# A hybrid attention layer on one core: the second and third products of every seven-product group change places, and the heads start with the gates

## The chip, the cores and the metric

The kernel runs on one core of one Trainium2 chip. The metric is the device time of one execution in microseconds (us); the time given for a kernel is the median of its runs. TensorE is written PE (its weight loads PEld), VectorE DVE, ScalarE ACT, GpSimd POOL, SyncE SP.

## The reference, cut to what matters

One layer, 256 tokens of 2048 features. The normalised input is multiplied by one wide matrix `w_in`. Its columns give, for each of four token mixers, queries, keys and values of 4 heads of 128, a path `z` and 2048 gate columns; an indexer gives the sparse mixer its top 64 keys.

```python
branches = (o_dsa, o_fox, o_diff, o_dil)          # four attentions, b = 0, 1, 2, 3
for b in range(N_BRANCHES):
    y = branches[b].reshape(bsz, seq, BRANCH_WIDTH) * jax.nn.silu(z_parts[b])
    term = jax.nn.sigmoid(g_parts[b]) * (y @ w_branch[b])
    merged = term if merged is None else merged + term
return x + merged @ w_out                          # then a last RMS norm
```

Everything is float32 and has to be nearly as exact: a matrix product is made of three products of rounded parts.

## The kernel before, in words

**Units.** All large products are cut into units of one weight tile (512 rows x 512 columns, 1 MB, `Raw`) each. `split_hi` (L195, ACT, the instruction at L207) rounds half a tile into `whi`; `split_lo` (L209, DVE, L220) subtracts that from the tile and gives `wlo`. A unit's matmuls (`three`, L378 to L380) take both. There are 8 buffers of `whi` halves and 6 of `wlo` halves, so splits run some three units ahead of PE. Six slots hold the tiles loaded by SP (L174); a slot is freed, and the next tile's load issued, when a tile's last `wlo` half is made.

**The order** is written out by hand: the list `units` (L1125 to L1162) is processed one by one in the loop at L1257. In unit i, for each half, the program issues a `wlo` half of a later unit, a `whi` half of a later unit, then the matmuls of the half. Then come the unit's `post` functions (they read finished PSUM banks), then, in some units, one round of the attention threads, then the threads that begin with this unit. Each engine executes its own instructions in the order in which the program issued them.

**Seven products.** `seven` (L448) computes two neighbouring blocks of 512 columns from 2048 features. Half of the features are handled as a 2 x 2 block product with seven products P1 to P7 (12 matmuls each), the rest by four plain units c2a, c2b, c1a, c1b (24 matmuls each). Four PSUM banks X, Y, Z, W accumulate. P5 uses the tile B12 to which POOL has added B11 by an accumulating DMA (`plus_dram`, L191; L180 to L193 hold `free`, `plus`, `plus_dram`). When P5's last `wlo` half has been made, DVE adds B22 to B12 (`plus`, L187) for P6, and a unit before P7's first split DVE subtracts B12 from B11 (again L187) for P7. P5 writes bank W, ACT reads it (`p5`, L540), then c2a goes on accumulating in W with its second row block (its first row block goes to Z). P3 writes Z.

**Stages.** For each mixer in the order b = 3, 2, 0, 1: one group of seven for queries and keys (`ps_qk`), one for `z` and values (`ps_zv`), two for the 2048 gate columns (`ps_g`, `gate_units`, 22 units), then 16 units that multiply the heads' output by `w_branch` (`ps_b`). At the end comes `w_out` (`ps_o`).

**Threads.** The attention is written as generators. A counter adds a unit's cost (12 in the groups of seven, 24 elsewhere) and a round is run when it has reached the `pace` in force (20; in the gate units 18, for b = 2 15). In a round every active thread goes on to its next `yield`, in the order in which the threads began. `qk_thread` turns queries and keys; `z_thread` makes SiLU(z): a sigmoid on ACT (L625), a product on DVE (L626), then transposes (L609) and copies (L611). `head_thread` and `diff_thread` (b = 2) make one head each: logits (L786), softmax on DVE (L798, L800, L803) with exponentials on ACT (L805), scaling (L821), transposes (L812 to L814), the copy `pt` on ACT (L816), the product with the values (L876 or L908), output `y` and its two parts `yT` (L828, L832, L833). Before, the heads begin right after the queries' group; `ready` (L835) holds them until `qk`, `index`, `fox` and `const` threads have ended, lets the first two heads (for b = 2 the first) go on and the others wait for `z_thread`; `values` (L849) holds a head until `z_thread` has ended. The tag `lg` of the softmax tile has 3 buffers. A unit with `need` first runs the named threads to their end: the first `w_branch` unit needs all heads of its mixer.

Of the kernel before, what the change touches and what calls it, by code (L numbers as in the profile page):

```python
# [112 lines left out]
def body(ctx: ExitStack, tc, x, norm_w, w_in, fox_b_f, lq1, lk1, lq2, lk2, subln_w,  # L113
# [8 lines left out]
    const = ctx.enter_context(tc.tile_pool(name="const", bufs=1))  # L122
# [192 lines left out]
    V = {}  # L315
    FIRST, LAST = 3, 1
# [129 lines left out]
                                    V["sf"][:, t, :, 0].bitcast(F32), op=ALU.subtract)  # L446

    def seven(src, c1, c2, base, ev, name, need={}, start=(),  # L448
              order="P1 P3 P5 c2a P6 c2b P7 P2 c1a P4 c1b", s0=0):

        st = {}
        p0 = 8 - s0
        order = order.split()
        apart = order.index("c2a") < order.index("P5")
        B11 = Raw(src, s0, 4, c1, 512)
        B12 = Raw(src, s0, 4, c2, 512, lead=4)
        B21, B22 = Raw(src, s0 + 4, 4, c1, 512), Raw(src, s0 + 4, 4, c2, 512)
        B12.then = lambda: plus_dram(B12, B11)  # L460

        def whole(half, k0):
            t = slice(half * P, (half + 1) * P)
            return lambda k: (base()[:, k0 + k, 0, t], base()[:, k0 + k, 1, t])

        def product_ps(bank):
            return att_ps(name) if bank == "V" else main_ps(name)

        def form(half, k0):
            return lambda k: (V["sf"][:, half, k0 + k, 0], V["sf"][:, half, k0 + k, 1])  # L470

        def product(bank, act, first=False):
            def mm(u, h):
                if first and h == 0:
                    st[bank] = product_ps(bank)
                for k in (2 * h, 2 * h + 1):
                    three(st[bank], act(k), u, k, first and k == 0, k == 3, on=True)
            return mm

        def plain(k0, two):  # L480
            def mm(u, h):
                for t, bank in enumerate(two):
                    new = bank not in st
                    if new:
                        st[bank] = main_ps(name)
                    act = whole(t, k0)
                    for k in (2 * h, 2 * h + 1):
                        three(st[bank], act(k), u, k, new and k == 2 * h, k == 3, on=True)
            return mm

        def c(k0, c0, two):
            return Unit(Raw(src, k0, 4, c0, 512), plain(k0, two))

        def read(f, bank, last=False):
            def g():
                f(st[bank])
                if last:
                    done(st[bank])
            return g

        def last_of(*names):
            return U[max(names, key=order.index)]

        Q = "V" if apart else "W"
        U = {
            "P1": Unit(B11, product("Y", whole(0, s0), True), [read(ev.p1, "Y")], frees=()),
            "P2": Unit(B21, product("X", whole(0, s0 + 4), True), frees=()),
            "P3": Unit(B22, product("Z", form(0, 4), not apart), frees=()),
            "P4": Unit(B21, product("Y", whole(1, s0 + 4)), frees=[B21], loads=()),
            "P5": Unit(B12, product(Q, form(1, 4), True), [read(ev.p5, Q)], frees=()),  # L510
            "P6": Unit(B12, product("Y", form(0, 0)), [read(ev.u2, "Y")], frees=(), loads=()),
            "P7": Unit(B11, product("Y", form(1, 0)), [read(ev.u3, "Y")], frees=[B11], loads=(),
                       pre=[lambda: plus(B11, B12, ALU.subtract)]),
            "c2a": c(p0, c2, "ZW"), "c2b": c(p0 + 4, c2, "ZW"),
            "c1a": c(p0, c1, "XY"), "c1b": c(p0 + 4, c1, "XY"),
        }
        U["P5"].after.append(lambda: plus(B12, B22))
        last_of("P3", "P5").after.append(lambda: free([B22]))
        last_of("P2", "P6").after += [lambda: plus(B21, B12), lambda: free([B12])]
        last_of("P3", "P6", "c2b").post.append(read(ev.c12, "Z", True))  # L520
        last_of("P7", "c2b", "P2").post.append(read(ev.c22, "W", True))
        U["c1b"].post += [read(ev.c11, "X", True), read(ev.c21, "Y", True)]
        U["c1b"].start += start
        for what, u in U.items():
            u.need += need.get(what, ())
            u.cost = 24 if s0 else 12
        return [U[what] for what in order]
# [57 lines left out]
    def qkvz_units(b, off, scale, start):  # L585


        def tok():
            return big.tile([P, 2, 512], F32, name="tok", tag="g", bufs=4)

        def dst_qk():
            if b == FIRST:
                both = big.tile([P, 2, 2, 512], F32, name="tok2", tag="y")
                V["q_"], V["k_"] = both[:, 0], both[:, 1]
            else:
                V["q_"], V["k_"] = tok(), tok()
            return V["q_"], V["k_"]

        def dst_zv():
            V["z_"] = tok()  # L600
            V["v"] = at.tile([P, 2, 512], F32, name="v", tag="v")
            return V["z_"], V["v"]

        def turn(src, dst, j0):
            for j in range(0, 4, 2):
                tp = att_ps("turn")
                for i in range(2):
                    for t in range(2):
                        nc.tensor.transpose(tp[:, i * S + t * P:i * S + (t + 1) * P],  # L609
                                            src[:, t, (j + i) * P:(j + i + 1) * P], ident)  # L610
                nc.scalar.activation(dst[:, j0 + j:j0 + j + 2],  # L611
                                     tp.rearrange("p (i s) -> p i s", i=2), AF.Copy)
                yield

        def qk_thread():
            V["qk"] = at.tile([P, 8, S], F32, name="qk", tag="qk")
            q_, k_ = V["q_"], V["k_"]
            yield
            yield from turn(q_, V["qk"], 0)
            yield from turn(k_, V["qk"], 4)  # L620

        def z_thread():
            z_ = V["z_"]
            sg = big.tile([P, 2, 512], F32, name="sg", tag="g", bufs=4)
            nc.scalar.activation(sg, z_, AF.Sigmoid)  # L625
            nc.vector.tensor_tensor(z_, z_, sg, op=ALU.mult)  # L626
            yield
            yield
            V["sz"] = at.tile([P, 4, S], F32, name="sz", tag="sz")
            V["v of"] = b  # L630
            yield from turn(z_, V["sz"], 0)

        sc = rsth if scale == HSCALE else rst8
        return (seven(w_in, off, off + 512, lambda: hT, Tok(dst_qk, sc, rst), "ps_qk",
                      start=[("qk", qk_thread)] + start, **(dict(
                          need={"P1": ["stack"], "P3": ["forms"]},
                          order="P1 P2 P3 P5 c2a P6 c2b P7 c1a P4 c1b") if b == FIRST else {}))
                + seven(w_in, O_Z + b * 512, off + 1024, lambda: hT, Tok(dst_zv, rst, rst),
                        "ps_zv", need={"c1b": ["qk"]}, start=[("z", z_thread)]))


    ki_hi = at.tile([P, S], F32R, name="ki_hi")
# [189 lines left out]
        nc.scalar.activation(yT[:, h, 0], y, AF.Copy)  # L832
        nc.vector.tensor_tensor(yT[:, h, 1], y, yT[:, h, 0].bitcast(F32), op=ALU.subtract)  # L833

    def ready(b, h, early):  # L835

        while any(a[0] in ("qk", "index", "fox", "const") for a in active):
            yield
        if h < early:
            for _ in range(2 * h):  # L840
                yield
        else:
            while V.get("v of") != b:
                yield
            for _ in range(h - early):
                yield
                yield

    def values(b):  # L849
        while V.get("v of") != b or any(a[0] == "z" for a in active):  # L850
            yield

    def head_thread(b, h):
        if h == 0:
            V["yT"] = big.tile([P, 4, 2, S], F32R, name="yT", tag="y")
        yield from ready(b, h, 2)
        ps = att_ps("lps")
        logits(ps, h, 0, P)
        if b == 0:
# [6 lines left out]
        nc.vector.reciprocal(r, r)  # L866
        yield
        scaled(e, r)
        yield from values(b)
        yield  # L870
        pt = transposed(e)
        yield
        o = att_ps("o")
        vs = slice(h * P, (h + 1) * P)
        v = V["v"]
# [4 lines left out]
    def diff_thread(b, h):  # L880
        if h == 0:
            V["yT"] = big.tile([P, 4, 2, S], F32R, name="yT", tag="y")
        yield from ready(b, h, 1)
        er = []
        for c in range(2):
            ps = att_ps("lps")
# [10 lines left out]
            nc.vector.scalar_tensor_tensor(e0[:, SL[t]], e1[:, SL[t]], r1[:, t:t + 1],  # L897
                                           e0[:, SL[t]], op0=ALU.mult, op1=ALU.add)
        yield
        yield from values(b)  # L900
        yield
        pt = transposed(e0)
        yield
# [3 lines left out]
        v = V["v"]  # L907
# [11 lines left out]
        for t in range(2):  # L919
            nc.vector.tensor_scalar(on[:, t * P:(t + 1) * P], o[:, t * P:(t + 1) * P],  # L920
                                    ms[:, t:t + 1], 1.0 - LAMBDA_INIT,
                                    op0=ALU.mult, op1=ALU.mult)
        yield
        yield
        yield
        ot = att_ps("otd")
# [211 lines left out]
    for b, off, scale, fn in ((3, O_DIL, HSCALE, head_thread), (2, O_DIFF, 0.125, diff_thread),  # L1138
# [3 lines left out]
        for i in range(2):  # L1142
            units += gate_units(b, i)
        for u in units[-22:]:
            u.pace = 15 if b == 2 else 18
        for n in range(4):
            units += branch_units(b, n)
        if b == 0:
# [7 lines left out]
    for n in range(4):  # L1156
        two[n].need.append(f"merge{n}")
    group = seven(w_out, 0, 512, lambda: V["mT"], Out(), "ps_o", s0=8, need={"P5": ["merge3"]},
                  order="c2a P1 P5 c2b P6 P2 P7 P3 c1a P4 c1b")
# [144 lines left out]
```

## Time and profile before

| | |
|---|---|
| median of 3 runs | 1042.16 us (1042.02 to 1044.82) |
| profiled execution | 1044.16 us, of which the span of the instructions is 1042.4 us |
| mean granted PE clock | 0.966 of full speed |
| busy: PE, DVE, ACT, POOL | 93%, 79%, 61%, 7% of the span |
| HBM | 204 GB/s over the span |

"Busy" of an engine counts its instructions' time; a wait line says which engine and source line waited, for which one, how long in all, how often, and the longest wait. The clock is the share of full speed that the throttle granted to PE.

### The profile page before, as it was taken

Reading aid. Unit: us, or ns where it says so; the run is one execution under the profiler, and the core shown is the slowest. Engines: PE = TensorE matmul, PEld = TensorE weight load, DVE = VectorE, ACT = ScalarE, POOL = GpSimd, SP = SyncE. Lnnn points to the kernel's source line nnn. Section 1 sums busy time; section 2 is a strip of 40 time slices with the busy share of each in tenths; the row PEclk is TensorE's granted clock in tenths of the full one; section 3 lists DMA queues with packets and bytes.
Section 4 is the critical chain, followed back from the end, with each engine's and each line's share of the span. In section 5 each row is a group of like instructions: output and inputs, shape, how many; then the busy total and the mean of one; then the engine's idle time right before and its main releaser. Section 6 shows DMA issues by size and latency. Waiting matters only on the chain. (4 is left out here: it accounts for less than half of the span.)

```text
span 1042.4 us, 12131 instructions
## 1 busy us (share of the span) xinstructions
PE 973.3 (93%) x4443; PEld 799.7 (77%) x4443; DVE 822.7 (79%) x967; ACT 634.7 (61%) x834; POOL 73.0 (7%) x84
## 2 busy tenths in 40 slices
PE   9988998999999989989999979799999797999897
PEld 8866886878878867778788858688788686887776
DVE  5888899978697877597888775887987767869992
ACT  5756676686456667676555665863666567544641
POOL 2011010000010000021100000001000000010220
PEclk9998999999999999989999989899999898999998
DMA  9949484747876938159895574388958562788132
GB/s 321 293 112 286 155 252 136 221 143 243 261 228 228 290 102 242 41 197 280 209 303 161 203 201 162 122 256 222 302 176 275 162 202 81 259 271 317 58 144 81
DMA packets 109019, 213.64 MB, mean 205 GB/s; under 512 B 8083, under 2 KB 10293, under 8 KB 108576
## 3 DMA queue, kind: packets, MB, share of 16 engines
q1 hardware_dynamic: 96240, 181.06, 50.1%
q0 software_dynamic: 12688, 31.80, 14.9%
q8 instruction: 35, 0.57, 0.2%
q14 instruction: 24, 0.20, 0.1%
q10 hardware_dynamic: 32, 0.01, 0.0%
HBM read 204.44 MB, written 8.41 MB: 204 GB/s over the span
## 5 line engine op out<-in xcount | busy, mean ns | idle before, releaser
L207 ACT ACTIVATE whi<-raw 128x1024 fp32r<-128x1024 f32 (+1 forms) x439 | 448.9, 1051 | 238.2 <-DVE raw L187 81.0
L220 DVE TENSOR_TENSOR wlo<-raw,whi 128x1024 fp32r<-128x1024 f32 (+1 forms) x439 | 525.6, 1224 | 84.3 <-PE ps_g L380 21.4
L378 PE MATMUL ps_g<-whi,hT 128*128 128x512 f32 x352 | 145.9, 415 | 25.9 <-ACT g L540 25.9
L380 PE MATMUL ps_g<-wlo,hT 128*128 128x512 f32 x352 | 141.9, 403 | 0.4 <-DVE wlo L220 0.4
L379 PE MATMUL ps_g<-whi,hT 128*128 128x512 f32 x352 | 142.2, 404 | 0.0
L187 DVE TENSOR_TENSOR raw<-raw 128x2048 f32<-128x2048 f32 x51 | 117.8, 2310 | 1.1
L378 PEld LDWEIGHTS ps_g<-whi,hT 128*128 128x128 f32 x352 | 69.6, 198 | 44.2 <-ACT g L540 28.4
L380 PEld LDWEIGHTS ps_g<-wlo,hT 128*128 128x128 f32 x352 | 69.1, 196 | 16.0 <-DVE wlo L220 0.8
L379 PEld LDWEIGHTS ps_g<-whi,hT 128*128 128x128 f32 x352 | 69.4, 197 | 14.0
L378 PE MATMUL ps_qk<-whi,hT 128*128 128x512 f32 x176 | 70.3, 399 | 6.9 <-ACT tok L540 6.9
L380 PE MATMUL ps_qk<-wlo,hT 128*128 128x512 f32 x176 | 69.5, 395 | 1.8 <-DVE wlo L220 1.8
L378 PE MATMUL ps_zv<-whi,hT 128*128 128x512 f32 x176 | 70.5, 400 | 0.5 <-ACT v L540 0.5
L379 PE MATMUL ps_qk<-whi,hT 128*128 128x512 f32 x176 | 69.6, 395 | 0.0
L380 PE MATMUL ps_zv<-wlo,hT 128*128 128x512 f32 x176 | 68.7, 390 | 0.0
L379 PE MATMUL ps_zv<-whi,hT 128*128 128x512 f32 x176 | 68.6, 390 | 0.0
L191 POOL DMA_DIRECT2D raw<-in_w_in_dram x16 | 21.1, 1316 | 503.5 <-DMA raw<-in_w_in_dram 191.1
L380 PE MATMUL ps_g<-wlo,sf 128*128 128x512 f32 x128 | 50.5, 395 | 2.3 <-DVE wlo L220 2.3
L378 PE MATMUL ps_g<-whi,sf 128*128 128x512 f32 x128 | 51.6, 403 | 0.0
L379 PE MATMUL ps_g<-whi,sf 128*128 128x512 f32 x128 | 50.3, 393 | 0.0
L378 PE MATMUL ps_b<-whi,yT 128*128 128x512 f32 x128 | 49.9, 390 | 0.0
L380 PE MATMUL ps_b<-wlo,yT 128*128 128x512 f32 x128 | 49.8, 389 | 0.0
L379 PE MATMUL ps_b<-whi,yT 128*128 128x512 f32 x128 | 49.8, 389 | 0.0
(266 smaller groups left out, 1567.3 us busy)
## 6 DMA issues: line engine op xcount, KB each, us to landing
raw<-in_w_in_dram SPq DMA_DIRECT2D x132, 1024.0 KB, 6.4
raw<-in_w_in_dram POOLq DMA_DIRECT2D x16, 1024.0 KB, 11.3
raw<-in_w_branch_dram SPq DMA_DIRECT2D x16, 1024.0 KB, 5.2
raw<-in_w_out_dram SPq DMA_DIRECT2D x16, 1024.0 KB, 5.8
md<-g POOLq DMA_DIRECT2D x12, 512.0 KB, 5.3
raw<-in_w_in_dram SPq DMA_DIRECT2D x7, 512.0 KB, 9.8
xs<-in_x_dram SPq DMA_DIRECT2D x8, 256.0 KB, 8.1
mp<-md POOLq DMA_DIRECT2D x4, 512.0 KB, 8.7
```

Source lines behind the costliest of these rows:

```text
L187: nc.vector.tensor_tensor(to.tile, of.tile, to.tile, op=op)
L191: nc.gpsimd.dma_start(to.tile.rearrange("p (k n) -> p k n", k=of.nk), of.src[of.k0 * P:(of.k0 + of.nk) * P, of.c0:of.c0 + of.n] .rearrange ...
L207: nc.scalar.activation(u.parts[0][h][:, s_], raw[:, s_], AF.Copy)
L220: nc.vector.tensor_tensor(u.parts[1][h][:, s_], raw[:, s_], u.parts[0][h][:, s_].bitcast(F32), op=ALU.subtract)
L378: nc.tensor.matmul(ps, ahi, u.hi(k)[:, cols], start=first, stop=False, skip_group_check=on)
L379: nc.tensor.matmul(ps, alo, u.hi(k)[:, cols], start=False, stop=False, skip_group_check=on)
L380: nc.tensor.matmul(ps, ahi, u.lo(k)[:, cols], start=False, stop=last, skip_group_check=on)
```

## The change

In every group of seven P5 comes second and P3 third (in the first group of all, where P2 stands second, P5 comes third and P3 fourth). The heads no longer begin behind the queries' group but at the last unit of the values' group, behind `z_thread`; that last unit needs `qk`, `fox` and `const` (for b = 0 also `index`) to have ended, so `ready` and `values` are gone. Head h waits 2h rounds from there. `head_thread` gets a second round between the copy `pt` and the product with the values; `diff_thread` loses one of three rounds behind the normalisation. The pace of the gates of b = 2 is 14.

```diff
     def seven(src, c1, c2, base, ev, name, need={}, start=(),
-              order="P1 P3 P5 c2a P6 c2b P7 P2 c1a P4 c1b", s0=0):
+              order="P1 P5 P3 c2a P6 c2b P7 P2 c1a P4 c1b", s0=0):
...
         return (seven(w_in, off, off + 512, lambda: hT, Tok(dst_qk, sc, rst), "ps_qk",
-                      start=[("qk", qk_thread)] + start, **(dict(
-                          need={"P1": ["stack"], "P3": ["forms"]},
-                          order="P1 P2 P3 P5 c2a P6 c2b P7 c1a P4 c1b") if b == FIRST else {}))
+                      start=[("qk", qk_thread)], **(dict(
+                          need={"P1": ["stack"], "P5": ["forms"]},
+                          order="P1 P2 P5 P3 c2a P6 c2b P7 c1a P4 c1b") if b == FIRST else {}))
                 + seven(w_in, O_Z + b * 512, off + 1024, lambda: hT, Tok(dst_zv, rst, rst),
-                        "ps_zv", need={"c1b": ["qk"]}, start=[("z", z_thread)]))
+                        "ps_zv", need={"c1b": ["qk", "fox", "const"] + ["index"] * (b == 0)},
+                        start=[z_thread] + start))
...
     def head_thread(b, h):
...
-        yield from ready(b, h, 2)
+        for _ in range(2 * h):
+            yield
...
         scaled(e, r)
-        yield from values(b)
         yield
         pt = transposed(e)
+        yield
         yield
         o = att_ps("o")
...
     def diff_thread(b, h):
...
-        yield from ready(b, h, 1)
+        for _ in range(2 * h):
+            yield
...
         yield
-        yield from values(b)
         yield
         pt = transposed(e0)
...
-        yield
         yield
         yield
         ot = att_ps("otd")
...
         for u in units[-22:]:
-            u.pace = 15 if b == 2 else 18
+            u.pace = 14 if b == 2 else 18
```

## Rows read from the trace of the kernel before

**Rows 1.** Part 1 of the page: busy us, share of the span, instructions

```profile
PE 973.3 (93%) x4443; PEld 799.7 (77%) x4443; DVE 822.7 (79%) x967; ACT 634.7 (61%) x834; POOL 73.0 (7%) x84
```

**Rows 2.** Waits of PE over the span: us in total, times, longest

```profile
PE ps_g L378 <- ACT g L540: 25.9, 6, 6.5
PE o L876 <- ACT pt L816: 14.6, 4, 6.7
PE ps_qk L378 <- ACT tok L540: 6.9, 4, 4.1
```

**Rows 3.** Gates of b=3, 2, 0, undisturbed stretch: us; busy PE, PEld, DVE, ACT, POOL; clock, DMA

```profile
166.60:266.00 99.40, 92.89 (x413) 75.92 (x412) 86.53 (x131) 69.14 (x98) 2.63 (x2) 0.97 0.63 193
374.80:487.20 112.40, 101.64 (x438) 80.78 (x437) 85.30 (x127) 78.76 (x127) 11.20 (x10) 0.92 0.57 174
594.70:702.90 108.20, 94.61 (x410) 77.50 (x409) 79.05 (x91) 68.99 (x94) 2.58 (x2) 0.92 0.58 177
676.00:702.00 26.00, 26.00 (x117) 21.52 (x116) 21.60 (x21) 15.36 (x18) 1.29 (x1) 1.00 0.83 257
```

**Rows 4.** Waits inside the gates of b=3, then b=2 (two), then b=0 (two)

```profile
PE ps_g L378 <- ACT g L540: 5.2, 2, 5.1
...
PE ps_g L378 <- ACT g L540: 8.4, 2, 5.1
PE ps_g L380 <- DVE wlo L220: 2.3, 1, 2.3
...
PE o L876 <- ACT pt L816: 6.7, 1, 6.7
PE ps_g L378 <- ACT g L540: 6.5, 1, 6.5
```

**Rows 5.** Stretches at clock 0.5: all ten, the first, and three pairs

```profile
sum 64.87, PE 47.98 PEld 38.76 DVE 57.64 ACT 41.01 POOL 7.72; mean PE 4.80 PEld 3.88 DVE 5.76 ACT 4.10 POOL 0.77
...
80.93:87.76 6.83, 5.16 (x12) 4.10 (x13) 6.75 (x11) 3.62 (x5) 2.66 (x3) 0.51 0.50 143
...
sum 13.66, PE 10.77 PEld 8.51 DVE 9.76 ACT 6.80 POOL 0.00; mean PE 5.38 PEld 4.25 DVE 4.88 ACT 3.40 POOL 0.00
...
sum 17.07, PE 8.79 PEld 7.52 DVE 14.71 ACT 14.18 POOL 0.00; mean PE 4.40 PEld 3.76 DVE 7.36 ACT 7.09 POOL 0.00
...
sum 10.24, PE 9.27 PEld 7.65 DVE 10.21 ACT 7.67 POOL 2.43; mean PE 4.64 PEld 3.83 DVE 5.10 ACT 3.84 POOL 1.22
```

**Rows 6.** Timelines of ACT and DVE, first gate group, b=2: start, us, instruction, idle before

```profile
380.34 0.67 ACT L537 ACTIVATE g<-ps_g,rst 128x512 f32<-128x512 f32 x1
381.03 1.28 ACT L625 ACT_TABLE_LOAD   x1
382.32 1.06 ACT L625 ACTIVATE sg<-tok 128x1024 f32<-128x1024 f32 x1
...
383.41 1.23 DVE L626 TENSOR_TENSOR tok<-tok,sg 128x1024 f32<-128x1024 f32 x1 [2.62 <-ACT sg L625]
...
388.07 1.06 ACT L207 ACTIVATE whi<-raw 128x1024 fp32r<-128x1024 f32 x1 [1.85 <-DVE raw L187]
389.03 0.67 ACT L540 ACTIVATE g<-ps_g,rst 128x512 f32<-128x512 f32 x1
```

**Rows 7.** Timelines of DVE and ACT, second gate group of b=0, fourth head

```profile
648.25 0.29 DVE L798 TENSOR_TENSOR lg<-lps,bias 128x128 f32<-128x128 f32 x1 [10.61 <-PE ptp L814]
...
649.96 1.28 ACT L805 ACT_TABLE_LOAD   x1 [10.18 <-DVE mx L803]
```

**Rows 8.** Groups by line: softmax on DVE, exponential on ACT

```profile
L800 DVE CUSTOM_DVE_ANT_0 lg<-lps,bias 128x256 f32<-128x256 f32 (+1 forms) x28 | 9.3, 363 | 17.6 <-PE ptp L814 12.7 <-PE lps L786 4.5
...
L805 ACT ACTIVATE lg<-lg,mx 128x128 f32<-128x128 f32 (+1 forms) x40 | 17.9, 448 | 24.2 <-DVE mx L803 24.2
```

**Rows 9.** Timeline of ACT before the first group of seven

```profile
58.42 0.64 ACT L414 ACTIVATE halves<-ps_iq 128x256 f32<-128x256 f32 x2
...
64.22 1.06 ACT L207 ACTIVATE whi<-raw 128x1024 fp32r<-128x1024 f32 x1 [1.79 <-DMA raw<-in_w_in_dram]
```

More of the change, by code (lines that the diff above doesn't have):

```diff
@@ L629, in z_thread @@
             V["sz"] = at.tile([P, 4, S], F32, name="sz", tag="sz")
-            V["v of"] = b
             yield from turn(z_, V["sz"], 0)
@@ L833, in put_y @@
         nc.vector.tensor_tensor(yT[:, h, 1], y, yT[:, h, 0].bitcast(F32), op=ALU.subtract)
-    def ready(b, h, early):
-        while any(a[0] in ("qk", "index", "fox", "const") for a in active):
-            yield
[L839 to L851, printed above, removed]
     def head_thread(b, h):
@@ L922, in diff_thread @@
                                     op0=ALU.mult, op1=ALU.mult)
-        yield
         yield
```

## The prediction, made before the changed kernel was run

> **What bounds the kernel now.** I read the page's busy times first: PE is busy 93% of the span [rows 1], so the time is PE's, and a change is worth what it does to PE's idle time and to its clock. Then the list of PE's waits: nearly all of it stands in three lines [rows 2]. 25.9 us are waits of gate matmuls for L540, ACT's reading of bank W behind P5, in six places; 6.9 us are the same wait in the queries' groups, 4.1 us of it once; 14.6 us are waits of the heads' product with the values for the copy `pt`. Then the stretches by stage. An undisturbed gate stretch has 117 matmuls in 26.00 us, 0.222 us each, so a unit of 12 takes 2.7 us and one of 24 5.3 us [rows 3]. The gate stages have a clock below 1, and DVE works 87%, 76% and 73% of them.
>
> The stretches at the low clock, 0.5 of full speed (1.2 GHz where 2.4 are possible), follow these waits, but for one behind a wait for `wlo` and one in the tail. PE works 47.98 us in the ten of them, which half a clock makes 24.0 us longer than needed [rows 5]. So a wait of 5 us here costs some 2.7 us more behind it.
>
> Why W is late is seen in the timeline of ACT [rows 6]. P5 has been done since about 383 us (389.03 + 0.67, less the wait of 5.1 [rows 4] and 1.3 us of matmuls in between), but ACT reads W only at 389.03: it works through the sigmoid of z and three splits, and before the last of its splits it waits until DVE has formed B11 - B12 (L187). The 1.3 us are the 6 matmuls of c2a's first row block; after them PE stands still.
>
> For the 14.6 us I read the fourth head of b=0 [rows 7]. DVE stands 10.61 us at its softmax, since the three `lg` tiles are still held by heads that wait for z; ACT waits 10.18 us for that softmax, and the copies `pt` of three heads, one round ahead of their use, come behind it.
>
> **The change, part by part.** The sum is made against the profiled execution, 1044.16 us, 2.0 above the median.
>
> *P5 before P3.* No instruction is added. The reading of W is issued one unit earlier, ahead of the split that waits for B11 - B12, and P3's 2.7 us now lie between P5 and c2a: the reading has 4.0 us where it had 1.3. B12 + B22 is formed one unit earlier too, so the splits for P6 wait less for it. P3 now takes the bank that P5 took (X of the group before) at the same place, so nothing new waits there. SP's order of loads stays as it is between groups of seven (B12 has a lead of 4 units, so moving P5 up by one puts it in a tie that the list resolves to the old order); behind the `w_branch` units B12 goes one load earlier and one branch tile one load later, which has three units, 16 us, to land. POOL's accumulating DMA is issued at the old places. I cost these at nothing; the cover is that lead.
>
> In the queries' groups of b=2, 0, 1 nothing else is on ACT, and the whole wait goes: 6.9 - 4.1 = **2.8 us**.
>
> In the gates it depends on the round of threads. In b=0 and 1 the first round falls behind the second unit, so the reading of W is issued ahead of it. There the waits go, 6.5 us [rows 4] and 25.9 - 5.2 - 8.4 - 6.5 = 5.8 us, and the low clock behind them, half of 10.77 us [rows 5]: **17.7 us**.
>
> In b=2 and 3 the first round falls behind the first unit. ACT then has, from P1's end: the reading of Y 0.67, table load and sigmoid 2.3, a wait for DVE's product 1.23 [rows 6], the first head's softmax, two of 0.36 and about 0.2, then (new in this place) a table load of 1.28 and two exponentials of 0.45 [rows 7, 8], two splits of 1.06, and the reading of W, 0.67: 10.1 us. PE wants W after P5, P3 and half a block, 2 x 2.7 + 1.3 = 6.7 us. So a wait of 3.4 us is left; with a split of DVE's in between I take 4.0 for b=2 (it is 5.1 now [rows 4]: **1.1 us** gained). In b=3 DVE is also still selecting keys; I take 5.5 for 5.1, **0.4 us** lost. Both keep their low clock.
>
> Here the table load deserves a look: it is 1.28 us, and its sigmoid starts right behind it, at 382.32 [rows 6]. The Trainium skill, "ScalarE: Activation LUTs", section "What ACT_TABLE_LOAD costs", speaks against the change here: it puts a switch at about 2.66 us with the drain. By that, two switches ahead of W would make both waits 2.8 us longer and the sum 5.6 us smaller; the row shows no such pause between L537's end and the sigmoid, so I keep 1.28.
>
> *Heads with the gates, one more round before the values.* The heads now follow each other by two rounds, `lg` tiles come free before the fourth head asks (in b=0, 1, 3), and `pt` has two rounds of at least 5 us in all for a copy of 0.5 us. The waits for `pt` go, 14.6 us, with the clock behind two of them, half of 8.79: **19.0 us**. What comes in their place: in the second gate group of b=0 and 1 the last head's softmax falls behind the unit ahead of P1, so ACT has two table loads (2.6), four splits (4.2), two readings (1.3) and exponentials (0.9), and about 4 us of sigmoids, copies and a wait for DVE before the reading of W, together 13 us against 3 x 2.7 + 1.3 + some 1 us of the heads' own matmuls, 10.5. Nothing in the trace shows this; it lies between 0 and the longest wait there, 6.7 us [rows 2]. I take the worked-out 3 us each, with 1.5 of clock: **9.0 us** lost.
>
> In the second group of b=2 the third and fourth head no longer bring their exponentials in front of W: 8.4 - 5.1 = 3.3 us, the wait of 2.3 us for `wlo` beside it [rows 4], and half of 9.27 us of clock [rows 5] go, **10.2 us**. Against that, DVE has 85.3 us of work in a stage that shrinks to about 101 [rows 3], and two softmaxes of b=2 still wait for an `lg` tile; I put **2.3 us** back, as much as the wait there now.
>
> The pace of 14 gives b=2 19 rounds in its 22 gate units instead of 17, and its last head needs 18, so no round has to be forced ahead of `w_branch`. No wait of PE stands there now; it costs and gives nothing, and without the new pace a round's few small instructions would lie bare.
>
> *The first group of all.* Here P5's first split moves ahead of the readings of the indexer's last product, and it waits for POOL's accumulating DMA, whose landing lets ACT go on at 64.22, while those readings begin at 58.42 [rows 9]. So ACT stops for up to 5.8 us, and DVE, which feeds PE from hand to mouth there, with it. The misc tile also loads after B12 instead of before. On the other side the 4.1 us wait for W and half of 5.16 us of clock can go, 6.7 us. Bounds +6.7 and -8.4 (5.8 and the clock); nearest is the row with the DMA, I take **0**.
>
> **The sum:** 2.8 + 17.7 + 1.1 - 0.4 + 19.0 - 9.0 + 10.2 - 2.3 = 39.1 us. 1044.2 - 39.1 = 1005.1, and 2.0 less for the median: **1003 us**.
>
> **The rivals.**
>
> *All waits go.* ACT's rounds are short enough after all. Then 25.9 + 14.6 + 6.9 + 2.3 us and up to 22 us of clock disappear, about 70: some 974 us. For it: ACT is at 64% in the gates of b=0. Against it: its work comes in lumps. Chance 0.14.
>
> *The exchange moves little.* PE does the same work ahead of c2a's second block, and if ACT is late by more than P3's 2.7 us everywhere, the gate waits for W stay near their size and only the waits for `pt` go, 19 us: 1023 us. Chance 0.16.
>
> *Slower: exponentials ahead of W.* With the heads in the gates, a softmax stands in ACT's queue before the reading of W in every one of the eight gate groups, and each loses as much as the worst one now, 6.5 us and 2.7 of clock: 74 us. Now the gates lose 25.9 + 14.6 + 2.3 and some 21 of clock, 64. Less the 2.8 us of the queries' groups the result is 7 us slower, 1049 us; it decides from about 8.4 us a group. For it: today's waits are of just this kind, and DVE is at 87% in the gates of b=3. Against it: only four of eight groups have a softmax at that place. Chance 0.12.
>
> **How the numbers follow.** The forecast has 0.58, with 985 to 1017 of its own from the bounds of the new waits (13 us either way together) and of the first group. The range, 980 to 1030, takes in the second rival and the upper end of the first, and leaves out the slower one and most of the first. A measurement of this kernel can tell 0.3%, 3 us, from no change. Faster: 0.58 + 0.14 + 0.12 of the second rival's 0.16 = 0.84; its weak end makes 0.04 for no change; slower 0.12.
>
> **What would show it.** Right: PE's list has no L876 and little of `ps_qk` L540; L540 in the gates is down from six places to about four, the longest in the first groups of b=3 and 2; five or six stretches at half clock are left; DVE's waits for L814 are gone in b=0 and 1. Wrong: L540 stands there with 20 us or more, `wlo` L220 becomes PE's main wait, or the first queries' group (60 to 119 us) grows by more than 8 us.

## The result, and the profile after

The median of 3 runs is 994.16 us (991.61 to 996.58) against 1042.16: a ratio of 0.9531 with the interval 0.9487 to 0.9576, 48.0 us less. The forecast was 1003 in a range of 980 to 1030. The profiled execution took 991.61 us, 52.55 less than that of before, and the stages below are compared between these two.

Part 1 of the page, to be held against [rows 1]:

```profile
PE 956.7 (97%) x4443; PEld 790.6 (80%) x4443; DVE 822.6 (83%) x967; ACT 632.3 (64%) x832; POOL 74.0 (7%) x84
```

The same matmuls, and PE is busy 16.6 us less: nearly all of that is time at the low clock (below). The rest of the gain is idle time, and the list of PE's waits (us in total, times, longest) says which:

```profile
PE ps_qk L378 <- ACT tok L548: 5.2, 1, 5.2
PE ps_g L378 <- ACT g L540: 3.6, 1, 3.6
PE rp L308 <- DVE qf L415: 3.2, 1, 3.2
...
PE otd L910 <- DVE on L903: 1.3, 1, 1.3
PE od L891 <- ACT pt L816: 1.0, 1, 1.0
PE ps_g L378 <- ACT g L548: 0.9, 1, 0.9
```

Of the three lines that were nearly all of it [rows 2], the 25.9 us for L540 in the gates are 3.6, in one place; the 14.6 us for `pt` and the 6.9 us of the queries' groups are gone (the product with the values stands at L859 now; it has no line). Two of the longest three are new: L548 and L415, both in the first group.

The stretches of the gates of b=3, 2, 0 and 1, as in [rows 3] (us; busy PE, PEld, DVE, ACT, POOL; clock, DMA share, GB/s):

```profile
172.20:270.00 97.80, 92.61 (x413) 76.27 (x412) 86.98 (x131) 71.77 (x100) 2.63 (x2) 0.97 0.65 201
375.30:476.50 101.20, 97.78 (x446) 76.79 (x446) 84.22 (x135) 75.55 (x131) 12.27 (x10) 1.00 0.61 182
581.80:671.10 89.30, 89.30 (x414) 74.52 (x413) 78.22 (x99) 70.54 (x99) 2.58 (x2) 1.00 0.69 212
776.40:865.70 89.30, 89.30 (x414) 74.52 (x413) 75.96 (x91) 70.78 (x99) 1.29 (x1) 1.00 0.68 222
```

In b=0 and 1 PE is busy for the whole 89.30 us at the full clock: nothing is left to gain there but work. Only b=3 still has a low clock. The three stretches at clock 0.50 in which PE still works, where [rows 5] had ten:

```profile
65.30:72.10 6.80, 5.65 (x12) 3.12 (x13) 5.93 (x9) 6.47 (x11) 0.00 (x0) 0.50 0.00 0
106.20:113.00 6.80, 5.87 (x14) 4.62 (x15) 4.76 (x8) 5.29 (x9) 0.00 (x0) 0.50 0.86 314
184.70:191.50 6.80, 5.40 (x13) 4.24 (x14) 6.59 (x17) 5.14 (x6) 1.33 (x1) 0.50 0.48 154
```

Each begins inside one of the three longest waits above. PE works 5.65 + 5.87 + 5.40 = 16.92 us in them, and half of it, 8.5 us, is lost to the clock where 24.0 were.

Stage by stage, gain in us by the forecast and by the stretches of the two traces:

| stage | forecast | measured |
|---|---|---|
| first group (queries and keys of b=3) | 0 | -6.2 |
| queries' groups of b=2, 0, 1 | 2.8 | 3.9 |
| gates of b=0 and 1 | 27.7 | 35.1 |
| gates of b=2 | 9.0 | 11.2 |
| gates of b=3 | -0.4 | 1.6 |
| the four values' groups | 0 | 4.5 |
| `w_branch`, and `w_out` at the end | 0 | 2.4 |
| sum | 39.1 | 52.5 |

(27.7 is the prediction's 17.7 + 19.0 - 9.0; 9.0 is 1.1 + 10.2 - 2.3.)

### The profile page after: what moved, and what is told of

Same layout as the page of the kernel before. It is cut to its first block, busy times and chain, and to the rows that moved or that the text cites. A ratio compares the mean times of both kernels' runs of the same rounds, so it can differ in the third digit from the quotient of the medians.

```text
span 989.9 us, 12129 instructions
## 1 busy us (share of the span) xinstructions
PE 956.7 (97%) x4443; PEld 790.6 (80%) x4443; DVE 822.6 (83%) x967; ACT 632.3 (64%) x832; POOL 74.0 (7%) x84
## 5 line engine op out<-in xcount | busy, mean ns | idle before, releaser
L220 DVE TENSOR_TENSOR wlo<-raw,whi 128x1024 fp32r<-128x1024 f32 (+1 forms) x439 | 526.8, 1225 | 71.0 <-issue 17.7
L378 PE MATMUL ps_g<-whi,hT 128*128 128x512 f32 x352 | 141.7, 402 | 4.6 <-ACT g L540 3.6
L380 PE MATMUL ps_g<-wlo,hT 128*128 128x512 f32 x352 | 138.2, 393 | 0.0
L379 PE MATMUL ps_g<-whi,hT 128*128 128x512 f32 x352 | 138.1, 392 | 0.0
L378 PEld LDWEIGHTS ps_g<-whi,hT 128*128 128x128 f32 x352 | 66.8, 190 | 20.5 <-ACT g L540 4.6
L380 PEld LDWEIGHTS ps_g<-wlo,hT 128*128 128x128 f32 x352 | 66.7, 189 | 14.2
L379 PEld LDWEIGHTS ps_g<-whi,hT 128*128 128x128 f32 x352 | 66.8, 190 | 13.3
```

The lines of the kernel that those rows point to most:

```text
L220: nc.vector.tensor_tensor(u.parts[1][h][:, s_], raw[:, s_], u.parts[0][h][:, s_].bitcast(F32), op=ALU.subtract)
L378: nc.tensor.matmul(ps, ahi, u.hi(k)[:, cols], start=first, stop=False, skip_group_check=on)
L379: nc.tensor.matmul(ps, alo, u.hi(k)[:, cols], start=False, stop=False, skip_group_check=on)
L380: nc.tensor.matmul(ps, ahi, u.lo(k)[:, cols], start=False, stop=last, skip_group_check=on)
```

## The experiments

Each ratio is against the kernel before, timed beside it on the same chip (medians 1043.0 to 1043.1 us; 1042.16 for the changed kernel).

### The two halves of the change, each alone

`order_alone` is the kernel before with the exchange of P5 and P3 and nothing else; `heads_alone` is the changed kernel with the old orders.

```diff
 order_alone, in before:
-order="P1 P3 P5 c2a P6 c2b P7 P2 c1a P4 c1b"
+order="P1 P5 P3 c2a P6 c2b P7 P2 c1a P4 c1b"
-need={"P1": ["stack"], "P3": ["forms"]}, order="P1 P2 P3 P5 c2a P6 c2b P7 c1a P4 c1b"
+need={"P1": ["stack"], "P5": ["forms"]}, order="P1 P2 P5 P3 c2a P6 c2b P7 c1a P4 c1b"
 heads_alone, in after: the same lines the other way
```

> The kernel before with the exchange of P3 and P5 alone; heads, rounds and pace as before. If the exchange takes away PE's waits for bank W (25.9 us in the gates, 2.8 in the later queries' groups, with some 13 us of low clock behind them) and the heads' part takes away the waits for pt (14.6 us and 4.4 us of clock), this run keeps the waits for pt, loses those for L540 in the gates but for a few us, pays some 6 us in the first queries' group, and comes to 1005 to 1012 us. If instead the heads' move is what frees ACT at that place, L540 stays above 15 us and the time above 1025 us.

> The changed kernel with P3 ahead of P5 again (heads with the gates, one more round, pace 14). By the first theory the waits for pt and DVE's waits for lg tiles are gone (19 us), PE's waits for L540 in the gates stay at 26 us or grow, since softmax and sigmoid now stand in front: 1018 to 1030 us. By the rival (the heads' move did it) L540 is below 10 us and the time 1000 us or less.

Measured: the order alone 1020.47 us, ratio 0.9779 (0.9758 to 0.98), 8 us above the upper end of what I expected; the heads alone 1023.28 us, 0.9809 (0.9791 to 0.9827), as expected. PE's waits, first with the order alone, then with the heads alone:

```profile
PE o L876 <- ACT pt L816: 18.8, 4, 8.0
PE ps_g L380 <- DVE wlo L220: 6.0, 3, 3.3
PE ps_qk L378 <- ACT tok L548: 5.2, 1, 5.2
PE ps_g L378 <- ACT g L548: 4.9, 3, 2.3
PE rp L308 <- DVE qf L415: 3.0, 1, 3.0
PE ps_g L378 <- ACT g L540: 2.6, 1, 2.6
```

```profile
PE ps_g L378 <- ACT g L540: 25.9, 8, 5.5
...
PE od L891 <- ACT pt L816: 2.7, 1, 2.7
```

The exchange takes the waits for W (25.9 to 2.6) and leaves those for `pt`; the heads take those for `pt` and leave 25.9 us for W (now in eight places instead of six). So each half takes the waits that the prediction gave it. It does not bring the gain in the stage where the prediction booked it. The gates of b=2, with the order alone and then with the heads alone (columns as in [rows 3]):

```profile
379.00:479.70 100.70, 94.84 (x437) 75.54 (x437) 81.90 (x126) 77.12 (x127) 8.87 (x10) 1.00 0.61 193
371.70:484.10 112.40, 102.30 (x445) 80.18 (x444) 86.69 (x135) 76.61 (x131) 13.11 (x10) 0.94 0.55 174
```

They took 112.40 us before and take 101.20 in the changed kernel: here the exchange alone brings the whole gain, and the heads alone bring none.

What I missed in the order alone is that the waits for `pt` grow, 14.6 to 18.8 us, and that waits for `wlo` and L548 in the gates are 10.9 us, where [rows 4] had 2.3. DVE still stands 31.7 us at its `lg` tiles there (20.6 and 11.1 at L800 and L798, for L814), and I take it that PE, with W on time, now runs into that. The halves gain 22.6 and 19.7 us, together 42.3, and the change 48.0; the difference is of the size of the intervals and I don't build on it.

### What the waits for `pt` came from

`lg4_before` gives the kernel before a fourth `lg` buffer (and takes one from `rel` for the room); nothing is moved. `one_round_pt` takes the second round before the values' product out of the changed kernel.

```diff
 lg4_before, in before:
-lg = at.tile([P, 384], F32, name="lg", tag="lg", bufs=3)
+lg = at.tile([P, 384], F32, name="lg", tag="lg", bufs=4)
-rel = at.tile([P, 2, S], F32, name="rel", tag="rel", bufs=2)
+rel = at.tile([P, 2, S], F32, name="rel", tag="rel", bufs=1)
...
 one_round_pt, in after:
         pt = transposed(e)
         yield
-        yield
         o = att_ps("o")
```

> The kernel before with four lg tiles instead of three (the room comes from the tag rel, one buffer instead of two, used only before the gates of b=3 end). Theory: DVE's waits of 10.6 us for an lg tile in the gates of b=0 and 1 make ACT, and so the copies pt, late; with a fourth tile these waits and PE's two long waits at L876 (13.3 us, with 4.4 us of low clock) go: 1021 to 1030 us. Rival: three heads bunched on one round are enough to make pt late; then L876 keeps 8 us or more and the time stays above 1035 us.

> The changed kernel with one round instead of two between the copy pt and the product with the values, as before the change. If the lg tiles held by waiting heads were the whole cause of the waits for pt, hardly any come back: 992 to 997 us and less than 3 us at L859 (the product with the values). If the second round is what hides the copy, PE waits 5 us or more at L859 and the time is above 998 us.

Measured: four buffers 1019.72 us, ratio 0.9771 (0.975 to 0.9791), a little below the range I expected; one round 995.06 us, 0.9545 (0.9521 to 0.957), which is not to be told from the changed kernel. With four buffers in the kernel before, PE's list has no line for `pt`, while the waits for W stand:

```profile
PE ps_g L378 <- ACT g L540: 24.1, 5, 6.5
...
PE ps_zv L378 <- ACT v L540: 3.5, 1, 3.5
```

So the waits for `pt` were a shortage of `lg` tiles, as read from the 10.61 us in [rows 7], and a buffer cures them as well as the later heads do (the wait at `ps_zv`, in a values' group of b=3 that is 4.7 us longer, came with the edit; I put it down to the single `rel` tile). It does more than that: the gates of b=2, where PE waited for no `pt`, take 102.8 us with it instead of 112.4. The second round, which the prediction counted as part of the cure, does nothing that shows.

### The first group, where 6.2 us were lost

`first_group_old` puts the first group alone back to P3 before P5. `lead5_alone` keeps the changed order everywhere and gives the load of B12 a lead of 5 units instead of 4, in every group. `first_old_lead5` does both.

```diff
 first_group_old, in after:
-need={"P1": ["stack"], "P5": ["forms"]}, order="P1 P2 P5 P3 c2a P6 c2b P7 c1a P4 c1b"
+need={"P1": ["stack"], "P3": ["forms"]}, order="P1 P2 P3 P5 c2a P6 c2b P7 c1a P4 c1b"
 lead5_alone, in after:
-B12 = Raw(src, s0, 4, c2, 512, lead=4)
+B12 = Raw(src, s0, 4, c2, 512, lead=5)
```

> The changed kernel with the first group of all in the old order P1 P2 P3 P5. Theory: its 6.2 us of growth come from P5's first split waiting for the accumulating DMA ahead of the indexer's evictions (ACT idle 6.8 us), and a second wait of 5.2 us at L548 from the same kind of wait of the next group's P5. Then PE's wait of 3.2 us for qf goes, a wait for W of some 4 us may come back, the L548 wait stays: stage of 61 to 65 us, time 990 to 994 us. Rival: the growth is DVE's saturation there; then the stage stays at 65 us or more.

> The changed kernel with B12 loaded with a lead of 5 units instead of 4, and its new order in the first group of all. If the second wait of the first stage (5.2 us at L548, with 6.8 us of low clock) is the accumulating DMA of the next group, this takes it away and leaves the first one (3 us for qf): first stage 58 to 62 us, 986 to 991 us. If the lead helped first_old_lead5 only together with the old first order, 992 to 997 us.

> As first_group_old, and B12 is loaded with a lead of 5 units instead of 4 in every group, so that its accumulating DMA starts earlier ahead of P5. If the L548 wait (5.2 us) is the next group's accumulating DMA landing late, it goes, with its stretch of low clock: first stage 57 to 61 us, 984 to 989 us. If that DMA is held by POOL or by the queue rather than by the load, nothing changes against first_group_old.

| kernel | us | ratio and interval | first group, us |
|---|---|---|---|
| changed | 994.16 | 0.9531 (0.9487 to 0.9576) | 65.4 |
| first_group_old | 987.41 | 0.9461 (0.9445 to 0.9477) | 59.1 |
| lead5_alone | 983.03 | 0.943 (0.9405 to 0.9455) | 58.6 |
| first_old_lead5 | 984.17 | 0.9429 (0.9415 to 0.9443) | 58.2 |

`first_group_old` and `lead5_alone` came out some 3 us below the ranges expected of them. `first_old_lead5` is 3.2 us below `first_group_old`, though no wait for L548 was left there for the lead to take, which its expectation had counted on. Of the 5.2 us between their profiled executions 0.9 lie in the first group, 1.5 in the gates of b=3, 2.1 at the end and 0.7 ahead of the first group; which of this is the lead's is not shown.

There are two waits in the first group of the changed kernel. The first is the one that the prediction bounded. ACT's timeline in the changed kernel:

```profile
56.65 1.04 ACT L207 ACTIVATE whi<-raw 128x1024 fp32r<-128x1024 f32 x1
64.52 1.06 ACT L207 ACTIVATE whi<-raw 128x1024 fp32r<-128x1024 f32 x1 [6.83 <-DMA raw<-in_w_in_dram]
65.48 0.64 ACT L414 ACTIVATE halves<-ps_iq 128x256 f32<-128x256 f32 x2
```

The split of P5 waits until 64.52 for POOL's accumulating DMA, and the readings of the indexer's product, which began at 58.42 before [rows 9], now stand behind it and begin at 65.48. PE gets 3.2 us of that (L415), and a low clock behind it.

The second wait, 5.2 us for L548, I had not seen coming, and my expectation for `first_group_old` was wrong about it too: I took it for a consequence of the exchange in the values' group, but it went with the first group's order. ACT's timeline 40 us on, in the changed kernel, shows the stop:

```profile
102.73 2.00 ACT L207 ACTIVATE whi<-raw 128x1024 fp32r<-128x1024 f32 x2 [8.43 <-DMA raw<-in_w_in_dram]
105.44 1.06 ACT L207 ACTIVATE whi<-raw 128x1024 fp32r<-128x1024 f32 x1 [0.72 <-DMA raw<-in_w_in_dram]
106.41 0.67 ACT L548 ACTIVATE tok<-ps_qk,rst 128x512 f32<-128x512 f32 x1
```

The DMA issues of 84 to 106 us (times, KB each, median us from issue to landing), first of the changed kernel, then with the lead of 5, say which transfer was late:

```profile
raw<-in_w_in_dram SPq DMA_DIRECT2D x5, 1024.0 KB, 12.8
raw<-in_w_in_dram POOLq DMA_DIRECT2D x1, 1024.0 KB, 10.4
bias<-vdr POOLq DMA_DIRECT2D x1, 512.0 KB, 11.8
```

```profile
raw<-in_w_in_dram SPq DMA_DIRECT2D x5, 1024.0 KB, 7.6
raw<-in_w_in_dram POOLq DMA_DIRECT2D x1, 1024.0 KB, 8.3
```

And POOL's timeline, in the same order, says why:

```profile
88.42 1.33 POOL L191 DMA_DIRECT2D raw<-in_w_in_dram  x1 [8.81 <-DMA raw<-in_w_in_dram]
89.21 1.31 POOL L320 DMA_DIRECT2D bias<-vdr  x1
```

```profile
86.56 1.32 POOL L191 DMA_DIRECT2D raw<-in_w_in_dram  x1 [29.58 <-DVE wlo L220]
87.33 1.10 POOL L334 DMA_DIRECT2D vdr<-vsb  x1
95.52 0.79 POOL L320 DMA_DIRECT2D bias<-vdr  x1 [7.08 <-DMA vdr<-vsb]
```

In the changed kernel the accumulating DMA, `bias` and `mask` (128 KB, at 89.99; both are attention tables that L320 reads back from `vdr`) leave POOL together, and SP's load of 89.78 us, 1 MB beside their 1.66 MB, takes 12.8 us: it lands at 102.6, and there ACT goes on. The accumulating DMA itself had landed at 98.8. In the kernel before these three also leave together, at 84.72, and the loads beside them take 12.1 us; 3.7 us later, because the first group is late, the same slow load is on the path. With a lead of 5 the accumulating DMA goes ahead of `vdr`, on which `bias` and `mask` wait, so these go 9 us after it; the loads take 7.6 us (median) and PE doesn't wait for L548. The load that took 12.8 us leaves even later there, at 90.84, but takes 6.9. So the second wait follows from the first group's delay and from POOL's transfers flying together; undoing either takes it away.

The two kernels with a lead of 5 price the first wait by itself. `lead5_alone` still has it, 4.3 us at L415, and its first group takes 58.6 us; `first_old_lead5` has 4.1 us of waiting for W in its place and takes 58.2. So the exchange in the first group costs 0.4 us by these two traces, and the second wait with its low clock is what made the group longer.

### The rivals tested, and the pace

`early_round` makes the first round in the gates of b=0 and 1 fall behind the first unit, as in b=2 and 3: it builds the slower rival's situation. `late_b3` delays the heads of b=3 by a round, `pace15` takes the old pace for b=2.

```diff
 early_round, in after:
             u.pace = 14 if b == 2 else 18
+        if b in (0, 1):
+            units[-22].cost = 18
 late_b3, in after (head_thread):
-        for _ in range(2 * h):
+        for _ in range(2 * h + (b == 3)):
 pace15, in after:
-            u.pace = 14 if b == 2 else 18
+            u.pace = 15 if b == 2 else 18
```

> The changed kernel with a first gate unit that counts 18 instead of 12 for b=0 and 1, so that the first round of threads (sigmoid, softmax, exponentials) falls behind P1, ahead of the reading of W, as it does for b=2 and 3. The prediction's slower rival prices that at 6.5 us of wait and 2.7 of clock a group, 18 us in all: 1012 us. If ACT gets through as in the gates of b=2 (no wait there), it is 0 to 2 us a group: 993 to 998 us.

> The changed kernel with the heads of b=3 one round later, so that the first softmax stands behind the reading of W. If that softmax, held up by DVE's selection of keys, is what keeps W waiting in the first gate group of b=3 (3.6 us, then 6.8 us of low clock), the wait goes and the time is 3 to 7 us shorter, 987 to 991 us. If ACT is late there because of DVE's other work, the wait stays and the time is 992 to 997 us.

> The changed kernel with the old pace of 15 in the gates of b=2: 17 rounds instead of 19, so that the last head's end is forced ahead of w_branch. Priced at nothing in the prediction but for bare small instructions: 993 to 997 us, with a gap of PE of 0 to 3 us at the start of w_branch of b=2. If the denser rounds are what keeps DVE's load level there, b=2's gates grow by 5 us or more.

`early_round`: 996.01 us, 0.9546 (0.9532 to 0.956). PE's line for W:

```profile
PE ps_g L378 <- ACT g L540: 4.1, 2, 3.6
```

That is 0.5 us more than the changed kernel's 3.6. In the first gate group of b=0 the exponentials now stand ahead of the reading of W (587.51 and 590.30 us). They cost next to nothing once P3 lies between, and the slower rival falls. `late_b3`: 993.03 us, 0.9522 (0.9506 to 0.9538), not to be told from the changed kernel. The wait for W in b=3 goes, and others come in the same stage:

```profile
PE ps_g L380 <- DVE wlo L220: 2.5, 1, 2.5
PE ps_g L378 <- DVE g L544: 1.9, 1, 1.9
```

Both are waits for DVE, which is busy 86.98 of that stage's 97.80 us in the changed kernel. The stage takes 96.4 us in this trace and has no low clock left; the median doesn't show that gain. `pace15`: 993.19 us, 0.952 (0.9503 to 0.9536): the pace is worth nothing that shows in the time, as costed. In its trace the gates of b=2 take 102.8 us instead of 101.2, with a wait of 3.3 us for L548 where 0.9 was.

### The best of them together

`lead5_late_b3` has the lead of 5, the first group in the old order and the later heads of b=3.

> first_old_lead5 (984.2 us) with the heads of b=3 one round later. In late_b3 the wait for W went and others came in its place in the same stage; if the wait for W there is worth its 3.8 us and half of a low-clock stretch, 979 to 982 us; if DVE's key selection only moves the wait elsewhere, 983 to 985 us.

982.24 us (5 runs, 981.09 to 984.79), 0.9431 (0.9406 to 0.9455): between the two expectations, and not to be told from `first_old_lead5` (0.9429), which lacks only the later heads, nor from `lead5_alone` at 983.03. The lead of 5 is the version to keep: one character, some 11 us below the changed kernel by the medians, with the interval of its ratio below the other's. Between the two profiled executions it is 6.8 us, all of it in the first group; where the rest of the 11 lies is not shown.

## Why the prediction was right, and which of its steps were off

**Right, and shown.** That the waits in the gates were W's reading held up on ACT: `heads_alone` keeps 25.9 us, `order_alone` 2.6. That the waits for `pt` were the three `lg` tiles: `lg4_before`. That a wait of some 5 us here brings some 2.7 us of low clock behind it: the three waits of 3.2 to 5.2 us that are left have 2.8, 2.9 and 2.7 us (half of 5.65, 5.87 and 5.40). That the pace and the first rounds are harmless: `pace15`, `early_round`. That b=3 keeps its wait for W: 3.6 us, where 5.5 were put. Of the signs named, DVE's waits for L814 are gone but for 1.9 us, but L540 stands in one place where about four were forecast, and PE works in three stretches at half clock where five or six were: in the gates of b=2, 0 and 1 the first rival, that all waits go, came nearer than the forecast.

**Mis-sized: "9.0 us lost" for new waits in the second gate groups of b=0 and 1.** Nothing was lost. I added up 13 us on ACT between the unit's end and the reading of W. ACT's timeline in b=0:

```profile
625.26 1.28 ACT L580 ACT_TABLE_LOAD   x1
...
629.32 1.28 ACT L805 ACT_TABLE_LOAD   x1
630.64 0.40 ACT L805 ACTIVATE lg<-lg,mx 128x128 f32<-128x128 f32 x1
...
636.27 0.67 ACT L540 ACTIVATE g<-ps_g,rst 128x512 f32<-128x512 f32 x1
```

All my items are there, but from the unit's end (626.9) to the end of L540 (636.9) it is 10.1 us, which the 10.5 us of PE's work cover (PE goes on in W at 638.1): the first table load ran before that end, while ACT had nothing to do, and the "about 4 us" of other work was an estimate on the high side.

**Mis-sized: the first gate group of b=2, a wait of 4.0 us and its low clock kept.** No wait is left. I had 10.1 us from P1's end to the reading of W; it is 7.3 (378.1 to 385.4):

```profile
378.27 0.69 ACT L537 ACTIVATE g<-ps_g,rst 128x512 f32<-128x512 f32 x1
378.85 1.05 ACT L625 ACTIVATE sg<-tok 128x1024 f32<-128x1024 f32 x1
379.92 1.28 ACT L805 ACT_TABLE_LOAD   x1
381.95 0.40 ACT L805 ACTIVATE lg<-lg,mx 128x128 f32<-128x128 f32 x1 [0.75 <-DVE mx L803]
...
382.84 1.99 ACT L207 ACTIVATE whi<-raw 128x1024 fp32r<-128x1024 f32 x2
384.74 0.66 ACT L540 ACTIVATE g<-ps_g,rst 128x512 f32<-128x512 f32 x1
```

Against [rows 6] the sigmoid L625 has no table load ahead of it, since no exponential runs in the values' group any more; and the exponential's load stands beside DVE's softmax, not behind it. The step failed because it counted a load that no longer runs and put the other durations end to end. It also had PE come to W too early, after 6.7 us: the first head's eight logit matmuls lie in between, and PE goes on in W at 387.0, 8.9 us after P1's end. In b=3 the same stretch holds a wait of 3.15 us for DVE's softmax, and the wait for W there is what is left:

```profile
178.16 1.28 ACT L805 ACT_TABLE_LOAD   x1
182.60 0.40 ACT L805 ACTIVATE lg<-lg,mx 128x128 f32<-128x128 f32 x1 [3.15 <-DVE mx L803]
...
185.38 0.67 ACT L540 ACTIVATE g<-ps_g,rst 128x512 f32<-128x512 f32 x1
```

The rule weighed in the prediction, that a switch of tables costs 2.66 us (the Trainium skill, "ScalarE: Activation LUTs", section "What ACT_TABLE_LOAD costs"), isn't borne out here either: the exponential starts 1.32 us after its load began (629.32 to 630.64), and ACT's work ahead of the load ends at 629.30.

The 2.3 us put back for DVE in b=2 were not needed, the wait for `wlo` is gone. All this would make b=2 8.9 us better than forecast, and it is 2.2: its heads bring 3.2 us of waits of their own (L910, L891, L548 above), and PE has 3.4 us more work there: 97.78 us at the full clock, where before 101.64 us, less the half of 5.20 + 9.27 us at the low clock, are 94.4.

**Booked on the wrong half: b=2's second gate group.** The 10.2 us there were to come from the third and fourth head, which "no longer bring their exponentials in front of W". With the heads alone the stage is as long as before: of the wait for W 1.9 us are left in the second group (3.3 before), a wait of 2.7 us for `pt` stands where the one of 2.3 us for `wlo` was, 6.8 of the 10.2 us at half clock stay, and the heads bring their extra work. With the order alone 11.7 us go. That the total of b=2 came out near is luck in this step.

**Failed: "POOL's accumulating DMA is issued at the old places. I cost these at nothing; the cover is that lead."** This made the 6.2 us lost in the first group. The term "0" of the exchange there held: the stop of ACT came as it was bounded (6.83 us of idle time, where 5.8 were put), the wait for W went against it, and the difference is the 0.4 us of the two kernels with a lead of 5. But the accumulating DMA of the next group is at its old place only in the program, not in time: it leaves 3.7 us later than before (88.42 for 84.72), with two other transfers, and a load that was just in time beside them no longer is. The sum had no term for that; the lower bound, 8.4 us, held it only by luck.

**Not foreseen:** the values' groups are 4.5 us shorter in sum, which I put down to the early heads' logits having left them; the heads alone take 3.4 us off these groups and the order alone 1.4. The 2.4 us at the end are not to be credited to the change: `w_out`, whose own order was not changed, takes from 99.7 (`order_alone`) to 104.6 us (`early_round`) in traces of kernels that leave that part alone. Of the 13.4 us by which the profiled execution beats the forecast's sum, the gates are 11.6 (7.4 + 2.2 + 2.0), the queries' groups 1.1, the values' groups and the end 6.9, less the 6.2. So the forecast's total is nearer than its terms: 19.6 us of gains too few stand against 6.2 of a loss that it did not have.

## What to carry to other kernels

A bank that an engine must read before the next product can go on wants a unit of other work between the two, as much as the reader's queue may be long; exchanging two steps can buy that without an instruction. When an engine's items ahead of a due time are added up, look which of them start before the data is there, and which must wait for another engine: the sum end to end was 10.1 us, and the stretches took 7.3 in b=2 and 11.2 in b=3. And where a step is moved in front of work that feeds the critical engine directly, ask for the transfer it waits for, and how many transfers leave beside that one.

## What the hardware did that I had not expected

A table load did not wait here for the data of the activation behind it: it began at 178.16 us, and 3.15 us of idle time lie between its end and its exponential. In the kernel before, at 649.96, one began only after the wait [rows 7]; what decides between the two was not tried.

A 1 MB load took 12.8 us beside three POOL transfers that were issued within 1.6 us, and the loads took 7.6 us where the accumulating one went 9 us ahead of the others. In the gates of b=2 of the changed kernel PE waited 1.3, 1.0 and 0.9 us at a clock of 1.00 throughout; its waits of 3.2, 3.6 and 5.2 us each brought a stretch at half clock.
